# Which engine forms the low parts of the weights, scales the delta rule's key products and makes the output's residual

## The chip, the cores and the metric

The kernel runs on one core of one Trainium2 chip. The metric is the device time of one execution in microseconds (us), as a median of several runs. Engines are named as in the profile: PE is TensorE's matmul, PEld its weight load, DVE is VectorE, ACT is ScalarE, POOL is GpSimd, SP is SyncE, which issues the DMAs.

## What is computed

One layer of a streaming encoder trunk, for 2048 prompt frames and 32 sample frames, 1024 wide. The normalised input `h` goes through one wide projection; its columns feed two branches, and the branches are merged, projected and added to `h`:

```python
qa, ka, va, za, qkv_b, zb, a_b, b_b, gate_a, gate_b = split_projection(x @ w_in)
ya = (oa.reshape(bsz, t, A_WIDTH) * jax.nn.silu(za)) @ w_branch_a   # oa: chunk-band softmax attention
yb = (ob * jax.nn.silu(zb)) @ w_branch_b                            # ob: gated delta rule, chunks of 64
mix = jax.nn.sigmoid(gate_a) * ya + jax.nn.sigmoid(gate_b) * yb
y = layer_norm(ALPHA * x + mix @ w_out, ln_g, ln_b)
```

The delta rule of branch B carries a 64x64 state per head from chunk to chunk:

```python
v_new = u_c - jnp.einsum('bhld,bhde->bhle', w_c, s)
o_c = (jnp.einsum('bhld,bhde->bhle', q_c * jnp.exp(gc_c)[..., None], s)
       + jnp.einsum('bhij,bhje->bhie', qk_c, v_new))
s = s * jnp.exp(g_last)[..., None, None] + jnp.einsum('bhld,bhle->bhde', k_dec, v_new)
```

## The kernel before

**The projection** runs as 49 jobs per half of the prompt (the sample frames ride with the second half). A job is a block of 128 columns of `w_in` (one job holds the 16 columns of `a` and `b`). To keep float32's accuracy in fast float16 matmuls, weights and `h` are both split into a high and a low float16 part, and a job multiplies high by high, low weights by high, and high by low (`multiply`). The weights' two parts are made per job by `divide`, half a tile (128x512) at a time: in the first half of the prompt ACT squares the tile, a matmul with a constant tile (`b<-w_sq,tiny`, in `power`) sums the squares over the partitions, and a power of two, `w_scale`, comes out; then ACT scales the raw tile in place (`wraw<-wraw,w_scale`, 128x1024), ACT casts each half to float16 (`whi`), and POOL subtracts that from the scaled tile (`wlo<-wraw,whi`, line 645).

**The order of the jobs** is fixed in `all_jobs`: a few jobs of the merge gates (`HEAD`), the `a`/`b` job, then `ORDER`: branch B's jobs (q, k, v, z of four pairs of heads) with gate jobs strewn in, then `TAIL` gate jobs, then branch A's. So the half of the prompt falls into a stretch with the delta rule (about 150 to 500 us and 950 to 1310 us) and one with attention (about 500 to 800 and 1310 to 1650). After 1650 us the branches are projected, merged and put through `w_out` in blocks of 256 frames (`merge`).

**The delta rule** (`phase_b`): DVE solves the triangular systems by substitution, 62 small operations per block of 512 frames (`substitute`, tiles `sys_t` and `sys_u`). Then `chain` steps through the chunks, two chains at a time: PE multiplies the state (`x<-state`), DVE forms `r` from it, PE multiplies `r` by the inverse (`x<-r`), DVE scales that by a factor per row (`vn<-x,sc`, line 1335), PE multiplies `vn` (`x<-vn`), and DVE updates the state (`state<-state,sc,x`). 132 such steps in all.

**The residual** (`x_load`): for each of 17 tiles of 128 rows (the last has 32), `xt` is fetched, DVE takes off the mean and multiplies by the inverse deviation (128x1024, two factors per row), and POOL multiplies by the row of gains and adds the row of offsets (`l0g`, `l0b`; for the first two tiles DVE does). In the same stretch `evac` and `fold` of `merge` do the gates on DVE (`sg<-sg,a`, `sg<-sg`), cast on ACT (`mh`), and leave the low part to DVE and POOL in turn (`ml`).

**What sets the order** on each engine is a planner inside the kernel. Every piece of work is a generator (a stream) with a clock; `Flow` always resumes the stream with the earliest clock, and the engine wrappers (`V`, `S`, `G`, `PE`) add a price per instruction and keep a busy time per engine (`Flow.spend`). The queues of the engines are what this yields, and each engine works its queue in order. A call on `nc.vector` instead of `V` goes into DVE's queue at that point but costs the plan nothing.

## Time and profile before

| | us |
|---|---|
| runs before, median of 3 | 2088.36 (2082.26, 2088.36, 2091.96) |
| profiled execution | 2083.65 |
| its span | 2081.6 |
| PE busy | 1968.6 (95%) |
| DVE busy | 1499.7 (72%) |
| ACT busy | 978.1 (47%) |
| POOL busy | 633.1 (30%) |

The span is the time from the first to the last instruction of the program in the profiled execution; 2 us of that execution lie outside it. Busy shares are means over the stages, and DVE's busy time holds time in which an instruction has started and stands still. The profiled execution is 4.7 us below the median of the runs.

### The profile page before, as it was taken

To read this page: it belongs to the slowest core of one execution; us is meant where nothing else is said; L and a number is where in the kernel's file an instruction comes from. 1 tells how busy PE (TensorE), PEld (TensorE's weight loads), DVE (VectorE), ACT (ScalarE), POOL (GpSimd) and SP (SyncE) were. 2 spreads that over 40 slices of the span, in tenths; PEclk is the share of its full clock that TensorE was granted. 3 is DMA by queue.
4 is the path that set the end of the run, shared out by engine and by line. 5 is a ranking of instruction groups with operands and counts; after the bars stand their busy time and mean duration, and the time that the engine had idled before them with its cause. 6 is when DMAs were issued, how large, how long until landed. Compare 5 with 4: busy or idle time off the path is not lost. (4 is left out here: it accounts for less than half of the span.)

```text
span 2081.6 us, 41386 instructions
## 1 busy us (share of the span) xinstructions
PE 1968.6 (95%) x15098; PEld 1411.3 (68%) x15098; DVE 1499.7 (72%) x4661; ACT 978.1 (47%) x2098; POOL 633.1 (30%) x708
## 2 busy tenths in 40 slices
PE   4999999999999999998999999999999988999998
PEld 3454666766465657566667777667666777888996
DVE  7679889873377758679998986356656667666775
ACT  5565554444466667564544543355656641111110
POOL 6244333422312113243332331311011134433342
PEclk9999999999999999999999999999999999999999
DMA  3233232323423233122233233332232445433331
GB/s 119 72 92 106 75 102 57 100 80 91 116 86 111 70 92 100 65 85 72 66 89 83 77 99 84 105 92 76 72 88 88 129 137 175 132 102 122 102 116 54
DMA packets 197719, 196.49 MB, mean 94 GB/s; under 512 B 79622, under 2 KB 147570, under 8 KB 197516
## 3 DMA queue, kind: packets, MB, share of 16 engines
q1 hardware_dynamic: 197516, 193.85, 31.6%
q8 instruction: 119, 1.95, 0.4%
q14 instruction: 84, 0.69, 0.1%
HBM read 135.91 MB, written 50.53 MB: 90 GB/s over the span
## 5 line engine op out<-in xcount | busy, mean ns | idle before, releaser
L260 PE MATMUL pj<-hi,whi 128*128 128x512 f16 (+2 forms) x1992 | 644.8, 339 | 10.4 <-DVE zb L260 2.7
L260 PE MATMUL pj<-hi,wlo 128*128 128x512 f16 (+2 forms) x1952 | 635.9, 338 | 2.4 <-POOL wlo L260 2.3
L260 PEld LDWEIGHTS <-whi 128*128 128x128 f16 x3984 | 413.5, 105 | 214.5 <-issue 3.9
L260 PE MATMUL pj<-lo,whi 128*128 128x512 f16 (+2 forms) x1992 | 457.7, 340 | 0.0
L260 POOL TENSOR_TENSOR wlo<-wraw,whi 128x512 f16<-128x512 f32 x192 | 226.9, 1184 | 585.9 <-ACT whi L260 313.0
L260 PEld LDWEIGHTS <-wlo 128*128 128x128 f16 x1952 | 204.8, 105 | 111.1 <-issue 10.7
L260 ACT CAST mh<-sg 128x256 fp32r<-128x256 f32 x64 | 25.9, 406 | 279.6 <-DVE sg L260 279.6
L260 ACT CAST ph<-b 128x512 f16<-128x512 f32 (+2 forms) x224 | 93.1, 421 | 100.0 <-PE b L260 96.8
L260 DVE TENSOR_TENSOR pl<-b,ph 128x512 f16<-128x512 f32 (+2 forms) x224 | 107.7, 485 | 44.7 <-ACT ph L260 43.1
L260 PE MATMUL a<-ghi,whi 128*128 128x256 f32 (+1 forms) x512 | 132.6, 290 | 6.3 <-DVE sg L260 6.2
L260 DVE TENSOR_TENSOR sys_u<-sys_u,sys_t 128x60 f32<-128x60 f32 (+23 forms) x527 | 129.3, 251 | 6.7
L260 ACT ACTIVATE wraw<-wraw,w_scale 128x1024 f32<-128x1024 f32 (+1 forms) x98 | 111.5, 1138 | 46.6 <-DVE w_scale L260 42.9
L260 PE MATMUL a<-ghi,wlo 128*128 128x256 f32 (+1 forms) x512 | 130.3, 285 | 0.0
L260 ACT CAST whi<-wraw 128x512 f16<-128x512 f32 (+1 forms) x196 | 119.4, 612 | 20.9 <-PE pj L260 18.0
L260 DVE TENSOR_TENSOR sys_t<-sys_u,sys_p 128x60 f32<-128x60 f32 (+21 forms) x459 | 121.2, 265 | 6.1
L260 ACT ACTIVATE sb<-sb,mx,unit 128x640 f32<-128x640 f32 (+4 forms) x128 | 108.8, 851 | 20.0 <-DVE mx L260 19.7
L260 DVE SCALAR_TENSOR_TENSOR acc<-raw,cwT,acc 128x512 f32<-128x512 f32 x144 | 114.0, 792 | 5.4 <-ACT acc L260 4.4
L260 POOL TENSOR_TENSOR w_scale<-w_scale,mhalf 128x1 f32<-128x1 f32 x49 | 30.9, 631 | 269.3 <-DVE w_scale L260 204.2
L260 PE MATMUL b<-ident,sb 128*128 128x128 f32 x560 | 100.6, 279 | 5.3 <-ACT sb L260 2.2
L260 PEld LDWEIGHTS a<-ghi,whi 128*128 128x128 f32 x512 | 98.0, 191 | 9.0 <-DVE sg L260 7.8
L260 ACT COPY v_t<-o 128x64 f32<-128x64 f32 x132 | 27.7, 210 | 161.1 <-PE o L260 133.3
L260 PEld LDWEIGHTS a<-ghi,wlo 128*128 128x128 f32 x512 | 97.8, 191 | 0.3
(350 smaller groups left out, 4221.8 us busy)
## 6 DMA issues: line engine op xcount, KB each, us to landing
wraw<-in_w_in SPq DMA_DIRECT2D x192, 256.0 KB
sg<-sig SPq DMA_DIRECT2D x112, 128.0 KB
sig<-sig SPq DMA_DIRECT2D x44, 256.0 KB
sys_p<-sol_p SPq DMA_DIRECT2D x17, 512.0 KB
x<-in_x_p SPq DMA_DIRECT2D x16, 512.0 KB
xt<-in_x_p SPq DMA_DIRECT2D x16, 512.0 KB
out_y_p<-xt SPq DMA_DIRECT2D x16, 512.0 KB
glo<-g SPq DMA_DIRECT2D x14, 512.0 KB
```

Source lines behind the costliest of these rows:

```text
L260: r = f(*a, **k)
```

## The change

Four edits:

- **Jobs get a mark, `delta`**: those of `ORDER` without the `a`/`b` job, the three `HEAD` jobs of the second half, and four of six `TAIL` jobs in each half: 25 jobs in the first half of the prompt, 28 in the second. The others (first jobs, branch A's, the last gates) are divided as before.
- **`divide` of a marked job**: ACT no longer scales the raw tile; it casts each half with the scale as a pointer operand (`whi<-wraw,w_scale`), and DVE forms the low half as scale times raw minus high (line 649 of the changed kernel) where POOL subtracted. The instruction is issued on `nc.vector`, and the plan books 0.7 us for it on a resource `W` of its own, not on DVE. In the first half the power sum's matmul is planned 1.0 us later.
- **`vn` of the chain** is formed by ACT, with the factor as its scale, not by DVE.
- **The residual** is formed by DVE alone, as subtract-then-multiply and multiply-then-add on halves of 512 columns (4 instructions per tile), with the row tiles as second tensor; POOL does none of it.

```diff
--- before.py
+++ after.py
@@ -575,7 +575,7 @@
         def __init__(self, half, wid, src, evac=None, key=None, cols=P, blocks=None):
             self.wid = wid
             self.half, self.src, self.evac, self.cols, self.key = half, src, evac, cols, key
-            self.end = self.two = False
+            self.end = self.two = self.delta = False
             self.blocks = blocks or BLOCKS[half]
 
     NRAW = 2
@@ -631,18 +631,28 @@
             yield t
             if job.half == 0:
                 S.activation(out=hi[:], in_=raw[:], func=AF.Square, accum_out=w_sq[:])
-                yield
+
+                yield flow.cur.clock + (1.0 if job.delta else 0.0)
                 yield from power(sc, w_sq[:])
                 flow.start(factors(job.wid))
             src, main = raw[:, :, 0:job.cols], hi[:, :, 0:job.cols]
-            S.activation(out=src, in_=src, func=AF.Copy, scale=sc)
+            if not job.delta:
+                S.activation(out=src, in_=src, func=AF.Copy, scale=sc)
             for i in range(2):
                 ks = slice(4 * i, 4 * i + 4)
-                S.copy(out=main[:, ks], in_=src[:, ks])
-                yield
 
                 rest_ = lo[:, ks] if job.cols == P else hi[:, ks, job.cols:P]
-                G.tensor_tensor(out=rest_, in0=src[:, ks], in1=main[:, ks], op=ALU.subtract)
+                if job.delta:
+
+                    S.activation(out=main[:, ks], in_=src[:, ks], func=AF.Copy, scale=sc)
+                    yield
+                    nc.vector.scalar_tensor_tensor(out=rest_, in0=src[:, ks], scalar=sc, in1=main[:, ks],
+                                                   op0=ALU.mult, op1=ALU.subtract)
+                    flow.spend("W", 0.7)
+                else:
+                    S.copy(out=main[:, ks], in_=src[:, ks])
+                    yield
+                    G.tensor_tensor(out=rest_, in0=src[:, ks], in1=main[:, ks], op=ALU.subtract)
                 if i:
                     raw_gate.give()
                     q_w.put((job, hi, lo))
@@ -1332,7 +1342,7 @@
                     flow.start(outputs(k.qb[:, c, :], st, os_))
                     yield
                     vn = bp.tile([P, HD], F32, tag=f"vn{xn}", bufs=2, name="vn")
-                    V.tensor_scalar(out=vn[:], in0=ys, scalar1=sc[:, 1, c:c + 1], scalar2=None, op0=ALU.mult)
+                    S.activation(out=vn[:], in_=ys, func=AF.Copy, scale=sc[:, 1, c:c + 1])
                     yield
                     PE.matmul(ds_, k.kdb[:, c, :], vn[:], start=True, stop=True)
                     flow.start(outputs(k.qkb[:, c, :], vn[:], os_, vc, k.out if c == k.nch - 1 else None))
@@ -1919,18 +1929,24 @@
 
     def all_jobs():
         for half in range(2):
-            for what in [None] * HEAD[half] + ["ab"] + ORDER:
+            for n, what in enumerate([None] * HEAD[half] + ["ab"] + ORDER):
                 if what is None:
-                    yield rest[half].pop(0)
+                    job = rest[half].pop(0)
+                    job.delta = half == 1 or n >= HEAD[0]
+                    yield job
                 elif what == "ab":
                     yield Job(half, 48, [(0, w_ab[:, :, 0:NH]), (32, w_ab[:, :, NH:2 * NH])], key=(1, None, 0), cols=HD,
                               blocks=AB_BLOCKS[half])
                 else:
                     p, i = what
                     wid = (16 + 4 * i if i < 3 else 28) + p
-                    yield Job(half, wid, [(0, w_in[wid])], key=(1, p, i))
-            for _ in range(TAIL[half]):
-                yield rest[half].pop(0)
+                    job = Job(half, wid, [(0, w_in[wid])], key=(1, p, i))
+                    job.delta = True
+                    yield job
+            for n in range(TAIL[half]):
+                job = rest[half].pop(0)
+                job.delta = n < TAIL[half] - 2
+                yield job
             for p in range(NP):
                 for i, f in enumerate((8, 4, 0, 12)):
                     yield Job(half, f + p, [(0, w_in[f + p])], key=(0, p, i))
@@ -2171,13 +2187,12 @@
         w.st = fp.tile([P, 2, 6], F32, tag="fst", bufs=3, name="fst")
         yield dma(xt[:rows], x_s if rows < P else x_p[gt * P:(gt + 1) * P, :])
         yield rows_ready
-        V.tensor_scalar(out=xt[:rows], in0=xt[:rows], scalar1=mv[:rows, gt, 0:1],
-                        scalar2=mv[:rows, gt, 1:2], op0=ALU.subtract, op1=ALU.mult)
-        yield
-        eng = V if gt < 2 else G
-        eng.tensor_tensor(out=xt[:rows], in0=xt[:rows], in1=rowv["l0g"][:rows], op=ALU.mult)
-        yield
-        eng.tensor_tensor(out=xt[:rows], in0=xt[:rows], in1=rowv["l0b"][:rows], op=ALU.add)
+        for name, q, op0, op1 in (("l0g", 0, ALU.subtract, ALU.mult), ("l0b", 1, ALU.mult, ALU.add)):
+            for c in range(2):
+                cs = slice(c * 512, (c + 1) * 512)
+                V.scalar_tensor_tensor(out=xt[:rows, cs], in0=xt[:rows, cs], scalar=mv[:rows, gt, q:q + 1],
+                                       in1=rowv[name][:rows, cs], op0=op0, op1=op1)
+                yield
         w.ready.done()
 
     def finish(w, gt, rows, c, ps, end):
```


Where it moves instructions. First VectorE's queue in the second half, beside one chunk's `r` (`sys_t` and `sys_u` are the substitution, `q_bd` and `v` belong to other blocks). Before:

```order
L260 TENSOR_TENSOR sys_t<-sys_u,sys_p 128x6x11
L260 TENSOR_TENSOR sys_u<-sys_u,sys_t 128x6x11
L260 TENSOR_TENSOR sys_t<-sys_u,sys_p 128x6x10
L260 TENSOR_TENSOR sys_u<-sys_u,sys_t 128x6x10
L260 TENSOR_TENSOR sys_t<-sys_u,sys_p 128x6x9
L260 TENSOR_TENSOR q_bd_10325<-qk_11413,ex 64x8x64
L260 TENSOR_TENSOR sys_u<-sys_u,sys_t 128x6x9
L260 SCALAR_TENSOR_TENSOR r<-x,negc,v_t_10363 128x64
L260 SCALAR_TENSOR_TENSOR v_12730<-e,acc 128x512
```

And after the change, at the same rows of the substitution:

```order
L260 TENSOR_TENSOR sys_t<-sys_u,sys_p 128x6x11
L260 SCALAR_TENSOR_TENSOR v_12647<-e,acc 128x512
L260 TENSOR_TENSOR sys_u<-sys_u,sys_t 128x6x11
L649 SCALAR_TENSOR_TENSOR wlo<-wraw,w_scale,whi 128x512
L260 SCALAR_TENSOR_TENSOR r<-x,negc,v_t_10335 128x64
L260 TENSOR_TENSOR sys_t<-sys_u,sys_p 128x6x10
L260 TENSOR_TENSOR sys_u<-sys_u,sys_t 128x6x10
L260 TENSOR_TENSOR sys_t<-sys_u,sys_p 128x6x9
L260 TENSOR_TENSOR sys_u<-sys_u,sys_t 128x6x9
L260 SCALAR_TENSOR_TENSOR state<-state,sc,x 128x64
```

A low part of the weights (L649), which stood in POOL's queue, now stands directly ahead of `r`, and `r` comes two rounds of the substitution earlier; 52 of the 106 such instructions stand between the first and the last chain step of a half, 18 of them at most two rows ahead of an `r` or a `state`.

Next ScalarE's queue, at the same block of the delta rule (`v_t<-o` copies a chunk's result out, `e` and `acc` are the convolution's, `zb` and `raw` empty a projection bank). Before, with the scaling of a whole raw tile and its two casts:

```order
L260 COPY k_bd_10309<-qk_12159 64x8x64
L260 ACTIVATE wraw<-wraw,w_scale 128x1024
L260 CAST whi<-wraw 128x512
L260 ACTIVATE zb<-pj,w_half 128x272
L260 ACTIVATE p_c_10360<-qk_12159 128x512
L260 COPY v_t_10363<-o 128x64
L260 CAST whi<-wraw 128x512
L260 COPY v_t_10363<-o 128x64 x2
```

After:

```order
L260 ACTIVATE vn<-x,sc 128x64
L260 COPY v_t_10335<-o 128x64
L260 ACTIVATE whi<-wraw,w_scale 128x512
L260 ACTIVATE raw_12506<-pj,w_inv 128x240
L260 ACTIVATE raws_12508<-pj,w_inv 128x32
L260 ACTIVATE vn<-x,sc 128x64
L260 ACTIVATE e<-acc 128x512
L260 ACTIVATE whi<-wraw,w_scale 128x512
L260 COPY v_t_10335<-o 128x64
L260 ACTIVATE vn<-x,sc 128x64
L260 COPY v_t_10335<-o 128x64
```

The scaling of the tile is gone, the cast carries the factor, and each chunk's `vn` stands among the other work, behind whatever is queued ahead of it.

Last VectorE's queue in one block of the merge. Before:

```order
L260 TENSOR_TENSOR ml<-sg,mh 128x256
L260 TENSOR_SCALAR xt<-xt,mv 128x1024
L260 SCALAR_TENSOR_TENSOR sg<-sg,a 128x256
L260 TENSOR_TENSOR sg<-sg 128x256
L260 SCALAR_TENSOR_TENSOR sg<-sg,a 128x256
L260 TENSOR_TENSOR sg<-sg 128x256
L260 TENSOR_TENSOR ml<-sg,mh 128x256
L260 SCALAR_TENSOR_TENSOR sg<-sg,a 128x256 x2
L260 TENSOR_TENSOR sg<-sg 128x256
```

After:

```order
L260 TENSOR_TENSOR ml<-sg,mh 128x256
L260 SCALAR_TENSOR_TENSOR xt<-xt,mv,l0g 128x512
L260 SCALAR_TENSOR_TENSOR sg<-sg,a 128x256
L260 TENSOR_TENSOR sg<-sg 128x256
L260 SCALAR_TENSOR_TENSOR sg<-sg,a 128x256
L260 SCALAR_TENSOR_TENSOR xt<-xt,mv,l0g 128x512
L260 TENSOR_TENSOR sg<-sg 128x256
L260 SCALAR_TENSOR_TENSOR xt<-xt,mv,l0b 128x512
L260 TENSOR_TENSOR ml<-sg,mh 128x256
L260 SCALAR_TENSOR_TENSOR xt<-xt,mv,l0b 128x512
```

The residual's halves (`xt<-xt,mv,l0g` and `l0b`) stand between the gates' instructions; POOL's queue has none of them left.

## Rows read from the trace of the kernel before

**Rows 1.** Busy time by stretch: us, each engine (instructions), TensorE clock, DMA share, GB/s.

```profile
150.00:500.00 350.00, 331.82 (x2493) 220.62 (x2492) 290.51 (x1091) 171.16 (x350) 118.79 (x150) 0.99 0.32 88
950.00:1310.00 360.00, 339.42 (x2987) 256.08 (x2987) 309.37 (x1133) 162.93 (x375) 112.30 (x147) 0.99 0.31 82
```

**Rows 2.** TensorE waits, 150 to 500 us: releaser, us in total, times, longest.

```profile
PE x L260 <- DVE r L260: 5.6, 6, 2.3
PE x L260 <- DVE state L260: 2.6, 5, 0.9
PE x L260 <- DVE vn L260: 2.4, 4, 0.9
```

**Rows 3.** TensorE waits, 950 to 1310 us.

```profile
PE x L260 <- DVE r L260: 9.0, 11, 1.4
...
PE x L260 <- DVE state L260: 2.2, 5, 0.8
...
PE x L260 <- DVE vn L260: 1.3, 4, 0.6
```

**Rows 4.** Timeline from 1045.8 us: start, us, engine, line, operation, tiles, [idle before, releaser].

```profile
1045.84 1.16 POOL L260 TENSOR_TENSOR wlo<-wraw,whi 128x512 f16<-128x512 f32 x1 [1.04 <-ACT whi L260]
1045.94 1.13 DVE L260 TENSOR_TENSOR sys_u<-sys_u,sys_t 128x60 f32<-128x60 f32 x1
...
1047.96 0.27 DVE L260 SCALAR_TENSOR_TENSOR r<-x,negc,v_t 128x64 f32<-128x64 f32 x1
...
1048.29 0.43 PE L260 MATMUL x<-r,u_bd 128*128 128x64 f32 x2 [1.43 <-DVE r L260]
```

**Rows 5.** Tiles sys_u and sys_t: count, duration ns min/median/max, first and last start.

```profile
L260 DVE TENSOR_TENSOR sys_u<-sys_u,sys_t x527: 147/211/1221, 143.7 to 1279.9; 128x60 f32<-128x60 f32 x17, 128x48 f32<-128x48 f32 x13, 128x66 f32<-128x66 f32 x11, 128x54 f32<-128x54 f32 x11
L260 DVE TENSOR_TENSOR sys_t<-sys_u,sys_p x459: 130/216/1224, 148.6 to 1279.7; 128x54 f32<-128x54 f32 x30, 128x72 f32<-128x72 f32 x17, 128x75 f32<-128x75 f32 x17, 128x60 f32<-128x60 f32 x17
```

**Rows 6.** The page, costliest groups: count, busy us, mean ns, idle before it.

```profile
L260 DVE TENSOR_TENSOR sys_u<-sys_u,sys_t 128x60 f32<-128x60 f32 (+23 forms) x527 | 129.3, 251 | 6.7
L260 DVE TENSOR_TENSOR sys_t<-sys_u,sys_p 128x60 f32<-128x60 f32 (+21 forms) x459 | 121.2, 265 | 6.1
```

**Rows 7.** Busy time of tile wlo alone, in the stretches with chain steps.

```profile
213.00:491.00 278.00, 88.32 (x231) 28.09 (x232) 0.00 (x0) 35.31 (x30) 0.98 0.32 86
993.00:1308.00 315.00, 113.06 (x379) 43.12 (x379) 0.00 (x0) 35.87 (x31) 0.99 0.31 82
```

**Rows 8.** Tile acc: VectorE's three-operand form with a pointer scalar, ns min/median/max.

```profile
L260 DVE SCALAR_TENSOR_TENSOR acc<-raw,cwT,acc x144: 711/744/1698, 87.4 to 1175.4; 128x512 f32<-128x512 f32 x144
```

**Rows 9.** VectorE's groups by shape: count, busy us, mean ns, idle before it.

```profile
L260 DVE TENSOR_SCALAR vn<-x,sc 128x64 f32<-128x64 f32 x132 | 37.0, 280 | 19.5 <-PE x L260 17.6
L260 DVE TENSOR_TENSOR sg<-sg 128x256 f32<-128x256 f32 x56 | 54.6, 979 | 0.8
```

**Rows 10.** ScalarE's groups by shape.

```profile
L260 ACT CAST whi<-wraw 128x512 f16<-128x512 f32 x192 | 118.0, 616 | 20.8 <-PE pj L260 18.0
L260 ACT ACTIVATE wraw<-wraw,w_scale 128x1024 f32<-128x1024 f32 x96 | 110.1, 1146 | 46.6 <-DVE w_scale L260 42.9 <-DVE rs L260 2.0 <-DVE sys_u L260 1.3
L260 ACT ACTIVATE acc<-raw,cwT 128x512 f32<-128x512 f32 x48 | 34.5, 719 | 15.2 <-DVE qk L260 7.5 <-DVE v L260 2.7 <-DVE qk_s L260 1.9
L260 ACT COPY v_t<-o 128x64 f32<-128x64 f32 x132 | 27.7, 210 | 161.1 <-PE o L260 133.3
```

**Rows 11.** TensorE's group of the weights' power sum, with what ended its waits.

```profile
L260 PE MATMUL b<-w_sq,tiny 128*128 128x1 f32 x98 | 17.1, 244 | 6.9 <-ACT whi L260 5.7 <-DVE kd_bd L260 1.2
```

**Rows 12.** ScalarE's waits, 950 to 1310 us.

```profile
ACT e L260 <- DVE acc L260: 30.9, 19, 3.6
```

**Rows 13.** Tile xt on GpSimd, and tile sg on VectorE, 1700 us to the end.

```profile
L260 POOL TENSOR_TENSOR xt<-xt,l0g x15: 2389/2395/2518, 1738.9 to 2034.3; 128x1024 f32<-128x1024 f32 x14, 32x1024 f32<-32x1024 f32 x1
L260 DVE TENSOR_TENSOR sg<-sg x61: 411/426/2607, 1704.1 to 2045.2; 128x256 f32<-128x256 f32 x53, 128x288 f32<-128x288 f32 x8
```

**Rows 14.** TensorE waits, 1738 us to the end.

```profile
PE a L260 <- DVE sg L260: 3.2, 3, 1.9
```


## The prediction

> **What bounds the kernel now.** I read the busy time by stretch first, then what TensorE waits for in the stretches that the change touches, then one such wait in the timeline. In both stretches with the delta rule PE is busy 95% and 94% of the time (331.82 of 350 us, 339.42 of 360) [rows 1]: PE is the bound, its matmuls stay the same, and the change can win only the 18.2 and 20.6 us in which PE stands still there, and the like elsewhere. DVE is busy 83% and 86% in the same stretches, ACT 49% and 45% [rows 1]. Of PE's 38.8 idle us, 10.6 in the first half (5.6 + 2.6 + 2.4) and 12.5 in the second (9.0 + 2.2 + 1.3), 23.1 in all, are waits of the chain's matmuls for DVE: for `r`, `state` and `vn` [rows 2, 3].
>
> Why DVE is late, one wait shows [rows 4]: POOL's subtraction for a weight tile starts at 1045.84 and takes 1.16 us; a small `sys_u` operation that DVE starts 0.10 us later takes 1.13 us and ends with it; `r` comes at 1047.96, and PE has stood for 1.43 us. The same tile's operations have a median of 211 ns and reach 1221, those of `sys_t` 216 and 1224 [rows 5]. So a DVE operation on two SBUF tensors stands while POOL works on such a subtraction. With the means of 251 and 265 ns [rows 6], 527 x 40 ns = 21.1 us and 459 x 49 ns = 22.5 us lie above the medians: 43.6 us of standing in these two groups, an estimate since their shapes differ. All groups together can't stand longer than POOL's subtractions last: 35.31 + 35.87 = 71.2 us in the two stretches with chain steps, 61 of them [rows 7].
>
> **The change part by part.** The sum is made against the profiled execution, 2083.65 us; the median of the runs is 4.7 us higher, and I add that at the end.
>
> *Low parts on DVE.* They leave POOL, and the 43.6 us of standing go with them. In their place come 106 operations with three operands and a pointer scalar on 128x512. `acc` is that form: 711 ns at least, 744 in the median [rows 8]; I take 744. In the changed order 52 of them stand between the first and the last chain step of a half: 52 x 0.744 = 38.7 us. The plan counts them on a resource of their own, not on DVE; neither did it count the standing. So 43.6 us of unplanned time on DVE become 38.7, in the same queue and ahead of the same `r` and `state`. The waits of 23.1 us scale to 23.1 x 38.7 / 43.6 = 20.5.
>
> *`vn` leaves DVE*: 132 x 0.280 = 37.0 us [rows 9]. DVE's load in the two stretches goes from 599.9 to 599.9 - 43.6 + 38.7 - 37.0 = 558.0 of 710 us, its free share from 15.5% to 21.4%. A late DVE catches up that much sooner, so I take 20.5 x 15.5 / 21.4 = 14.8 us. Saved: 23.1 - 14.8 = **8.3 us**. The ends are 0 (the new operations delay as the old standing did, and the plan, which knows that `vn` is gone, packs the steps closer) and 23.1 (every wait goes).
>
> *On ACT*, per marked job, the scaling of 1.146 us goes, and two casts grow from 0.616 us to 0.719, the price of `acc<-raw,cwT`, which carries a pointer scale [rows 10]: 53 x (1.146 - 0.206) = 49.8 us less. `vn` adds 132 of 128x64 from PSUM: the plain copy of that shape takes 0.210 us, with the same 0.103 for the pointer 0.313, so 41.3 us more. ACT's load stays. What counts is how long `vn` takes after its matmul. The instruction is 33 ns longer than on DVE, 132 x 0.033 = 4.4 us if PE stood for every one; PE waited at 8 of the 132 [rows 2, 3]. An engine's queue costs a late comer about its busy share times half an instruction: ACT's mean is 171.16 / 350 = 0.49 us, so 0.49 x 0.245 = 0.12 us; DVE's is 290.51 / 1091 = 0.27 us, so 0.83 x 0.135 = 0.11 us [rows 1]. That is even. I take **+1 us**, between 0 and 4.4; the case of a blocked queue is a rival below.
>
> The Trainium skill, *ScalarE: Activation LUTs*, "Rules for kernel authors", speaks against this edit: it gives adding and multiplying to VectorE, not ScalarE. Its figures in "What ACT_TABLE_LOAD costs" (186 ns, 0.833 per element, 93 per pointer operand) make an estimate of 332 ns for this `vn`, which would put 6.9 us in the place of the 4.4. The rows here show a smaller difference, 0.313 against 0.280, and a DVE that is fuller than ACT, so I keep the rows.
>
> *The power sum 1.0 us later.* PE stood 5.7 us in front of it for ACT's squares, in the first half of the prompt [rows 11]. An added microsecond of planned distance covers most waits of that size, though not those ahead of unmarked jobs: **-3 us**, between 0 and -5.7.
>
> *The residual.* POOL's multiplications with `l0g` take 2.4 us each and start at 1738.9 us [rows 13]; the gates' `sg<-sg` on DVE has a median of 426 ns but reaches 2607 [rows 13], with a mean of 979 over 56 [rows 9]: 56 x 0.553 = 31 us of standing in one group. That goes. DVE gets four operations per tile of about 0.74 us, 17 x 4 x 0.74 = 50 us at most, where it had one pass of the tile. It is a fair trade for DVE, and for PE only 3.2 us of waits for `sg` lie after 1738 us [rows 14], part of them at the start, where POOL isn't the cause. I take **-2 us**, between 0 and -3.2.
>
> Raw tiles come free earlier and the weights' parts are ready sooner, since a step of 1.146 us is gone; PE hardly waits for them now, so this costs and gives nothing. Elsewhere the new order shifts work by a few instructions; I take 0. The two delta stretches show a granted clock of 0.99 [rows 1], 7 us at most to win or lose with fewer or more stops.
>
> Sum: -8.3 + 1 - 3 - 2 = -12.3, so 2083.65 - 12.3 = 2071.4, and with 4.7 for the median **2076 us**.
>
> **The rivals.**
>
> 1. *One for one.* The new operations on DVE delay the chain just as the standing did: 18 of the 52 stand at most two rows ahead of an `r` or a `state`, and the plan reckons with none. Then the 23.1 us stay, and only -3 - 2 + 1 is left: 2083.65 - 4 + 4.7 = 2084 us. For it: unplanned time falls only from 43.6 to 38.7 us. Against it: the standing may be up to 71.2 us, and DVE loses 37 us of other work.
>
> 2. *All of it.* The standing is what made PE wait, and without it the plan holds: -23.1 - 5.7 - 3.2 = -32 us, so 2083.65 - 32 + 4.7 = 2056 us. For it: the wait in the timeline has POOL's operation right ahead of it [rows 4]. Against it: the new operation takes 0.74 us in the same place, where the standing took 1.13 - 0.21 = 0.92. The Trainium skill, *SBUF — State Buffer*, "Who interferes with whom", says that a VectorE instruction with two SBUF inputs and a GpSimd instruction that reads SBUF exclude each other for the whole instruction. By that rule the trace agrees (1.13 us beside 1.16), all standing behind a subtraction ends, but the new operation, with two SBUF inputs itself, can be held by what POOL still does.
>
> 3. *Slower: `vn` gets stuck in ACT's queue.* ACT works in order, and it stands at the convolution's tanh until DVE has made `acc`: 19 times in the second half's stretch, 30.9 us, 1.6 us each [rows 12]. A `vn` behind such an instruction stands as long, and so does its chain. With as many in the first half, 38 x 1.6 = 62 us; if half of them have a `vn` behind them, PE loses 31 us against the 5 that the other edits give: 2083.65 + 31 - 5 + 4.7 = 2114 us. It decides from 15 us on, that is when one in four does. Against it: after `r` the next step was as exposed to DVE's own queue before.
>
> **How the numbers follow.** A measurement of this kernel can tell about 0.5% (10.4 us) from no change; the runs before lie 9.7 us apart. Chances: the forecast 0.41, one for one 0.28, all of it 0.17, slower 0.14. Faster by over 0.5% means under 2078: all of rival 2 and 0.33 of the forecast, together 0.50. Within 0.5%: 0.08 of the forecast, 0.27 of rival 1, 0.02 of rival 3, together 0.37. Slower: 0.01 and 0.12, together 0.13. The range goes from rival 2's 2056 to 2096: rival 1 plus the 4.4 us of `vn` and the 7 us of clock; beyond it lie most of rival 3 and little of rival 2, under 0.2.
>
> **What would show it.** In the profile after: PE's waits for `r` and `state` in the two stretches near 13 us, and for a `vn` on ACT near 2; the maximum of `sys_u` and `sys_t` seldom above 1 us and their means near the medians; the new `wlo` on DVE at 0.71 to 0.75 us; `sg<-sg` near 0.43 us; the wait for the squares under 3 us. I am wrong if `r` waits as long as before with a `wlo` right ahead of it (rival 1), if waits for `vn` on ACT exceed 15 us (rival 3), or if PE's idle time moves elsewhere, into waits for weights or at the changes of stretch.

## The result, and the profile after

| | median us | runs | ratio to before, 95% interval |
|---|---|---|---|
| before | 2087.93 | 13 (2077.27 to 2091.96) | |
| after | 2094.38 | 13 (2090.52 to 2101.38) | 1.0043 [1.0031, 1.0056] |

The change makes the kernel slower by 0.43%, 9 us by the ratio. That is less than the 0.5% that I called no change, and inside my range, but on the other side of zero from the forecast of 2076. The profiled execution took 2101.26 us (span 2099.5), 7 us above the median; the one of before took 2083.65. Below, every time is given as ratio x 2087, as microseconds above or below before, since each group of runs had its own runs of before beside it.

In the two stretches with the delta rule nearly all went as forecast. TensorE's waits (releaser, us, times, longest), 150 to 500 us and then 950 to 1310 us, against [rows 2, 3]:

```profile
PE b L260 <- ACT p_c L260: 6.2, 2, 5.7
PE x L260 <- DVE state L260: 5.6, 6, 2.1
PE x L260 <- ACT vn L260: 1.4, 2, 0.8
...
PE x L260 <- DVE r L260: 0.9, 3, 0.4
```

```profile
PE x L260 <- DVE r L260: 4.4, 9, 1.1
PE x L260 <- DVE state L260: 3.8, 6, 0.9
```

`r`, `state` and `vn` together fall from 23.1 to 16.1 us, where I had forecast 14.8 and 1 for `vn`. The page's groups (count, busy us, mean ns, idle before), and under them two of the groups by shape, answer to [rows 6, 9, 10, 11]:

```profile
L260 DVE TENSOR_TENSOR sys_u<-sys_u,sys_t 128x60 f32<-128x60 f32 (+23 forms) x527 | 112.4, 218 | 7.8
...
L260 DVE TENSOR_TENSOR sys_t<-sys_u,sys_p 128x60 f32<-128x60 f32 (+20 forms) x459 | 99.5, 219 | 6.7
...
L260 ACT ACTIVATE whi<-wraw,w_scale 128x512 f16<-128x512 f32 x106 | 75.5, 716 | 45.9 <-DVE w_scale L260 27.3
L260 ACT ACTIVATE vn<-x,sc 128x64 f32<-128x64 f32 x132 | 41.2, 312 | 119.1 <-PE x L260 118.4
```

```profile
L260 DVE TENSOR_TENSOR sg<-sg 128x256 f32<-128x256 f32 x56 | 26.7, 477 | 0.7
```

```profile
L260 PE MATMUL b<-w_sq,tiny 128*128 128x1 f32 x98 | 16.1, 233 | 2.3 <-ACT whi L260 1.9 <-DVE ss L260 0.4
```

`sys_u` and `sys_t` lose most of their standing (means 251 and 265 before, now 218 and 219), the cast takes 716 ns (forecast 719), `vn` 312 (forecast 313), `sg<-sg` 477 instead of 979, and the squares keep PE for 1.9 us instead of 5.7. The new `wlo` on DVE has a median of 745 ns (forecast 744).

And yet the time rose. The busy time by stretch (engines, granted clock, DMA share, GB/s) shows where; first after, then the one stretch of before that [rows 1] leaves out:

```profile
150.00:500.00 350.00, 331.30 (x2483) 224.30 (x2482) 279.08 (x1081) 170.70 (x394) 76.41 (x111) 0.96 0.32 87
800.00:950.00 150.00, 129.67 (x990) 88.00 (x989) 104.42 (x229) 82.64 (x166) 23.92 (x48) 0.93 0.24 74
950.00:1310.00 360.00, 343.85 (x2974) 255.18 (x2972) 308.14 (x1129) 166.27 (x415) 76.39 (x123) 0.99 0.30 82
```

```profile
800.00:950.00 150.00, 143.29 (x1111) 98.75 (x1110) 110.13 (x247) 96.78 (x190) 58.03 (x85) 0.99 0.26 82
```

Between 800 and 950 us, where one half of the prompt gives way to the other and no chain step runs, PE is busy 13.6 us less, at a granted clock of 0.93 instead of 0.99. From 150 to 500 us it is busy as long as before, but the clock is 0.96 instead of 0.99, up to 10.5 us over 350. That part can't be laid to the marks or the clearing: e1 and e6 (below) have the same instructions in the same order on every engine up to 800 us, at a clock of 0.98 and 0.99, and the last `x<-r` of the first half starts at 506.4 us in after, 499.5 in e1 and 497.8 in e6. So some 7 to 9 us of this one execution, itself 7 us above the median, come from neither. The first chain step of the second half starts at 1040 us, 29 us later than before's 1011; from there to the end after is 11 us faster.

Most of the 13.6 us is one wait. DVE's timeline and then PE's after (start, us, engine, line, operation, tiles, [idle before, releaser]):

```profile
850.32 0.91 DVE L260 MEMSET k_bd<- 128x1024 f32 x1 [0.16 <-issue]
...
867.50 0.91 DVE L260 MEMSET u_bd<- 128x1024 f32 x1 [0.16 <-issue]
868.33 1.28 DVE L649 SCALAR_TENSOR_TENSOR wlo<-wraw,w_scale,whi 128x512 f16<-128x512 f32 x2
```

```profile
857.88 0.38 PE L260 MATMUL pj<-hi,whi 128*128 128x512 f16 x1
869.01 0.61 PE L260 MATMUL pj<-hi,wlo 128*128 128x512 f16 x1 [10.75 <-DVE wlo L649]
```

When the second half opens its buffers, DVE clears 17 diagonal tiles, 1.07 us from one to the next, 850.3 to 868.4 us. The low parts of the first two marked tiles of that half were formed before it (809.9 to 822.8 us); the third marked tile has both of its low parts behind the clearing in DVE's queue, and PE stands 10.75 us for them. Before, DVE cleared from 838.9 to 856.9 us, and POOL formed the two low parts of that tile beside it, at 842.1 and, here in its timeline, at 845.2; PE waited 0.38 us for the second:

```profile
845.24 1.16 POOL L260 TENSOR_TENSOR wlo<-wraw,whi 128x512 f16<-128x512 f32 x1 [1.94 <-ACT whi L260]
```

The other new wait is 5.7 us for `p_c` at 192 us. Two lines of ACT's timeline and one of DVE's show its source: DVE stands 3.81 us for a transfer (`sys_p`), `sc` is queued behind it, ACT stands 4.28 us for `sc`, and `p_c` comes last of what queued up on ACT.

```profile
188.38 0.21 ACT L260 ACTIVATE sc<-sc 128x8 f32<-128x8 f32 x1 [4.28 <-DVE sc L260]
...
191.69 0.61 ACT L260 ACTIVATE p_c<-qk 128x512 f32<-128x512 f32 x1
```

```profile
186.76 0.24 DVE L260 TENSOR_SCALAR sys_t<-sys_p,sys_u 128x31 f32<-128x31 f32 x1 [3.81 <-DMA sys_p<-sol_p]
```

### The profile page after: what moved, and what is told of

It is laid out like the page before. It is cut to its first block, busy times and chain, and to the rows that moved or that the text cites. A ratio compares the mean times of both kernels' runs of the same rounds, so it can differ in the third digit from the quotient of the medians.

```text
span 2099.5 us, 41323 instructions
## 1 busy us (share of the span) xinstructions
PE 1979.9 (94%) x15098; PEld 1418.5 (68%) x15098; DVE 1474.8 (70%) x4682; ACT 969.1 (46%) x2177; POOL 437.0 (21%) x572
## 5 line engine op out<-in xcount | busy, mean ns | idle before, releaser
L260 PE MATMUL pj<-hi,whi 128*128 128x512 f16 (+2 forms) x1992 | 651.0, 341 | 14.7 <-POOL whi L260 3.5
L260 PE MATMUL pj<-hi,wlo 128*128 128x512 f16 (+2 forms) x1952 | 643.3, 342 | 13.6 <-DVE wlo L649 10.8
L260 POOL TENSOR_TENSOR wlo<-wraw,whi 128x512 f16<-128x512 f32 x86 | 99.5, 1160 | 345.0 <-issue 199.0
L260 DVE TENSOR_TENSOR sys_u<-sys_u,sys_t 128x60 f32<-128x60 f32 (+23 forms) x527 | 112.4, 218 | 7.8
L260 DVE SCALAR_TENSOR_TENSOR acc<-raw,cwT,acc 128x512 f32<-128x512 f32 x144 | 108.6, 754 | 6.8 <-ACT acc L260 5.7
L260 DVE TENSOR_TENSOR sys_t<-sys_u,sys_p 128x60 f32<-128x60 f32 (+20 forms) x459 | 99.5, 219 | 6.7
L260 ACT ACTIVATE whi<-wraw,w_scale 128x512 f16<-128x512 f32 x106 | 75.5, 716 | 45.9 <-DVE w_scale L260 27.3
L260 ACT ACTIVATE vn<-x,sc 128x64 f32<-128x64 f32 x132 | 41.2, 312 | 119.1 <-PE x L260 118.4
L260 DVE CUSTOM_DVE_ANT_0 sb<-a,bias 128x320 f32<-128x320 f32 (+4 forms) x128 | 61.8, 486 | 44.8 <-PE a L260 43.9
```

Source lines behind the costliest of these rows:

```text
L260: r = f(*a, **k)
```

## Experiments

Theory A: the loss is the marking of the second half's first three tiles, whose low parts stand behind the clearing. Rival B: `vn` on ACT and low parts on DVE stop PE more often in the first half. Rival C: any new order of the instructions brings such stops. (The expectations speak of 20 cleared tiles and of the first of the three; the trace shows 17, and the third.)

### The three tiles and the clearing

**e1**, the changed kernel without these marks:

```
-                    job.delta = half == 1 or n >= HEAD[0]
+                    job.delta = n >= HEAD[half]
```

> The changed kernel, but the first three weight tiles of the second half of the prompt stay unmarked: POOL forms their low parts, as in the kernel before. Theory A (the loss sits at the change of halves: the low part of the first of these tiles stands on DVE behind the clearing of 20 tiles at about 0.9 us each, PE stops once for 10.8 us there and runs part of the next stretch at the lower clock): the wait for wlo near 869 us goes, the window 800 to 950 us gets back about 14 us of PE idle time and some 6 us of clock, and the time falls by 12 to 20 us from the changed kernel's 2094, to 2074 to 2082. Theory B (the loss is spread: vn on ACT and low parts on DVE make PE stop more often in the first half, where the granted clock fell from 0.99 to 0.96): the time stays at 2088 to 2096, whatever happens at 869 us. Theory C (the loss is what any new order of the instructions can bring, tied to no part): the time moves by a few us in either direction, and the stretches that the edit doesn't touch change as much as the one that it does.

Measured: 0.9948 [0.9931, 0.9965], 10.9 us faster than before and 19.9 faster than after. From the last `x<-r` of the first half to the first of the second, after takes 533.7 us and e1 514.1, 19.6 less: the whole gain lies there. The stretch, beside after's 129.67 and 0.93:

```profile
800.00:950.00 150.00, 144.33 (x1123) 100.14 (x1121) 119.98 (x276) 91.34 (x182) 39.95 (x71) 0.99 0.26 81
```

**e5**, the kernel before with these three tiles marked and nothing else changed (`job.delta = half == 1 and n < HEAD[1]`, `vn`, residual and power sum as before):

> The kernel before with one thing alone: the first three weight tiles of the second half are marked, so DVE forms their six low parts and ACT scales in the cast; all other tiles, vn, the residual and the power sum as before. Theory A (a low part that stands on DVE behind the clearing of 20 tiles stops PE): one PE wait for wlo of about 11 us near 855 us, the granted clock in 800 to 950 us at 0.93 instead of 0.99, nothing won elsewhere: 2085 + 11 + 6 = 2102, between 2096 and 2106. Theory C (new order as such): within 5 us of 2085, with no long wait.

Measured: 1.0083 [1.0069, 1.0098], 17.3 us slower. PE's longest wait between 800 and 950 us:

```profile
PE pj L260 <- DVE wlo L649: 13.2, 1, 13.2
```

**e6**, the changed kernel, all tiles marked, the clearing of the second half on POOL:

```
-                V.memset(t[:], 0.0)
+                (G if half else V).memset(t[:], 0.0)
```

> The changed kernel, all its tiles marked, but in the second half POOL clears the 20 diagonal tiles, not DVE. Theory A in its narrow form (the clearing ahead of the low part on DVE is the cause, not that DVE forms it): the wait near 869 us shrinks to under 1 us and the time comes down like that of the kernel with the three tiles unmarked, to 2072 to 2082. Rival (DVE is a worse place for the low parts of these tiles whatever stands ahead): the time stays above 2088.

Measured: 0.9971 [0.9959, 0.9983], 6.1 us faster than before, 15.1 faster than after. POOL's and DVE's timelines:

```profile
844.26 3.64 POOL L260 MEMSET qk_bd<- 128x1024 f32 x4
847.84 2.75 POOL L260 MEMSET q_bd<- 128x1024 f32 x3
```

```profile
845.50 0.75 DVE L649 SCALAR_TENSOR_TENSOR wlo<-wraw,w_scale,whi 128x512 f16<-128x512 f32 x1 [5.13 <-ACT whi L260]
```

In e6 PE works the same matmuls in the same order as in after, to the end, so the two traces can be laid side by side: at the same matmul after is 10.6 us behind just ahead of its stop, 22.9 us behind at 872.4 us and 22.6 at the last matmul. So the stop and the first matmuls behind it cost 12.4 us, and the rest of the way adds nothing; 9.8 of the 10.6 us were there before the clearing began, in the same queues.

Theory A holds from three sides: marking the three tiles costs 17 us alone, 20 in the changed kernel and 28 between e16 and e3 (below), and it is the clearing ahead of two of the six low parts, not their being on DVE, that costs. The stop is 11 to 13 us of it; where the rest comes from stays open. The clearing on POOL doesn't stretch the low part beside it: 0.75 us, its median. The Trainium skill, *SBUF — State Buffer*, "Who interferes with whom", says that a VectorE instruction with two SBUF inputs contends with a GpSimd instruction that reads SBUF, not with one that only writes it; these two rows agree.

**e17**, the changed kernel with the low parts booked on DVE in the plan (`V.scalar_tensor_tensor`, where the change issues them past the plan and books 0.7 us on a resource "W" that no engine has):

> The changed kernel, the same instructions on the same engines, but the plan counts the low parts on DVE instead of on a resource of their own. If the booking is the cause: the plan sees the first low part of the second half come late, puts other work on PE ahead of it, and the wait near 869 us falls to under 3 us: 2076 to 2084. If the clearing's place is the cause (all clearings are issued in one go, so nothing can go between them, and the weight tiles are multiplied in order): the wait stays at 10 to 13 us, 2088 to 2100.

Measured: 1.0107 [1.0093, 1.0122], 22.3 us slower than before, 13 slower than after, at a clock of 0.970 to 0.974. The wait is 13.2 us again. The booking isn't the cause of the stop: the kernel issues the clearings in one go, and nothing goes between them. The time is above the 2088 to 2100 that I expected of this case. **e18**, the same booking in the fastest kernel (e11, below):

> The fastest kernel so far (low parts on DVE but for the first three tiles of the second half, residual on DVE, vn on DVE, no later power sum: 2064) with the low parts booked on DVE. If unplanned time on DVE still delays the chain of the delta rule there: 2054 to 2060. If PE's waits for r, state and vn (16 us in the two stretches) are what the chain's length leaves in any order: 2060 to 2070.

Measured: 0.9945 [0.9931, 0.9958], 10.6 us slower than without the booking. Both halves of what I expected from honest booking failed; new stops came elsewhere (`v_t` on POOL 4.9 us, `vf` on ACT 4.6), and why the unbooked order is better stays open.

### The parts alone

**e3**, low parts with all their marks, alone (`vn`, residual and power sum as before):

> The kernel before with one part alone: low parts of the marked weight tiles on DVE and the scaling in ACT's casts; vn stays on DVE, the residual on POOL, the power sum's planned distance as before. Theory A: the stop of about 11 us at the change of halves is there, and the time is above the kernel before by 5 to 12 us (11 us of stop and some 6 of clock, less what r and state win, which my sum put at 20.5 of 23.1 left, so 3): 2093 to 2100. Theory B (vn on ACT is the cause): no loss, 2080 to 2088. Theory C: a few us either way.

Measured: 1.0053 [1.0033, 1.0072], 11.1 us slower, with a wait for `wlo` of 11.5 us at 861. As A said. **e16**, the same without the three marks:

> The kernel before with low parts on DVE and the scaling in ACT's casts alone, the first three tiles of the second half left to POOL; vn, the residual and the power sum as before. By the runs so far (2064 with the residual, which alone is worth 11.6): 2073 to 2077, a gain of 9 to 13 us. By my prediction's working (waits from 23.1 to 20.5): 2082 to 2084. In the trace the waits for r and state in the two stretches with the delta rule should then be near 8 us in all by the first, near 18 by the second.

Measured: 0.9921 [0.9904, 0.9939], 16.5 us faster, more than either figure. PE's busy time in the two stretches:

```profile
150.00:500.00 350.00, 333.19 (x2488) 221.78 (x2485) 292.02 (x1130) 156.26 (x334) 78.19 (x112) 0.98 0.32 89
...
950.00:1310.00 360.00, 343.66 (x3018) 259.52 (x3017) 297.64 (x1157) 149.40 (x357) 73.09 (x112) 0.99 0.31 84
```

PE stands still for 16.8 and 16.3 us there, 5.6 less than before [rows 1]. The waits for `r`, `state` and `vn` are 9.5 and 8.3, 5.3 less. For `r` and `state` alone, of which I expected near 8 or near 18, they are 12.8: between the two, and the time is below both. The span of the profiled execution is 11.4 us shorter than before's: 5.6 of idle time in the two stretches, 1.2 between 800 and 950 us (144.48 us busy), and 4.6 in small pieces elsewhere. The median gained some 5 us more than this one execution.

**e7**, the residual alone:

> The kernel before with one part alone: the output's residual as four operations with three operands on DVE, none on POOL. My sum gave it 2 us of gain, between 0 and 3.2: 2080 to 2085 with the kernel before at 2084. If low parts and vn bring nothing and the residual is what wins in the kernel with the three tiles unmarked (2075): 2076 to 2079. The stretch from 1700 us on is the only one that may change in its operations; a change ahead of that would be order alone.

Measured: 0.9942 [0.9926, 0.9958], 12.1 us faster. Up to 1661 us PE has the same matmuls in the same order, within 2.2 us of before; from the first `a<-ghi` matmul to the last matmul PE takes 401.5 us instead of 412.4. Before and then alone, nearly that stretch:

```profile
1661.00:2073.00 412.00, 395.72 (x2554) 350.06 (x2552) 282.37 (x494) 74.94 (x191) 152.04 (x122) 0.98 0.37 118
```

```profile
1662.00:2063.00 401.00, 389.39 (x2553) 348.65 (x2552) 268.75 (x541) 75.14 (x191) 79.21 (x92) 0.99 0.37 121
```

The same matmuls take 6.3 us less busy time, of which the clock (0.98 to 0.99) can be 4, and 4.7 us less idle time. DVE, which does POOL's work on top, is busy 13.6 us less: `sg<-sg` falls from 979 to 466 ns.

**e4**, `vn` on ACT alone:

> The kernel before with one part alone: vn on ACT, 132 times. Theory A: DVE loses 37 us of work in the two stretches with the delta rule, the waits for r and state fall by some us, and nothing stops at the change of halves: 2080 to 2088. Theory B: p_c waits some 5 us more on ACT, the clock in the first half falls as in the changed kernel, and the time rises by 5 to 10 us to 2093 to 2098. Theory C: a few us either way.

Measured: 1.0038 [1.0023, 1.0052], 7.9 us slower. **e9**, the same move without telling the plan, so that every queue keeps the order of before:

```
-  V.tensor_scalar(out=vn[:], in0=ys, scalar1=sc[:, 1, c:c + 1], scalar2=None, op0=ALU.mult)
+  nc.scalar.activation(out=vn[:], in_=ys, func=AF.Copy, scale=sc[:, 1, c:c + 1])
+  flow.spend("V", 0.125 + HD / 960.0)
```

> The kernel before with vn on ACT, but counted by the plan as if it stayed on DVE: every engine's instructions keep the order of before, and only vn changes its engine. (With the plan told, vn alone made 2093, 8 us more than before.) If what that kernel lost comes from vn's place on ACT (a vn behind other ACT work): about 2093 here too, with waits for vn on ACT above the 3.7 us of before. If it comes from the plan's new order, which has no room for what it doesn't count: 2078 to 2085, and waits for r and state smaller than 14.5 and 4.8 us, since DVE has 37 us less to do in the same order.

Measured: 1.0035 [1.0020, 1.0051], 7.3 us slower, in the old order. Its waits, and ACT's timeline ahead of one of them:

```profile
PE x L260 <- ACT vn L1335: 17.0, 24, 1.5
...
PE x L260 <- DVE r L260: 11.8, 11, 4.2
PE x L260 <- DVE state L260: 6.5, 12, 1.3
```

```profile
309.38 1.15 ACT L260 ACTIVATE wraw<-wraw,w_scale 128x1024 f32<-128x1024 f32 x1 [0.47 <-DVE w_scale L260]
310.56 0.62 ACT L260 CAST whi<-wraw 128x512 f16<-128x512 f32 x1
311.09 0.62 ACT L260 ACTIVATE p_c<-qk 128x512 f32<-128x512 f32 x1
311.74 0.32 ACT L1335 ACTIVATE vn<-x,sc 128x64 f32<-128x64 f32 x1
```

My third rival, at half its size: `vn` makes PE wait 17.0 us instead of 3.7, here (1.42 us) behind the scaling and the cast of a weight tile and a `p_c`, while `r` gets only 2.7 us back. In e4 the plan knew of the move, and PE hardly waits for `vn` (0.2 us), although ACT still scales: the plan decides on these waits. The loss is as large all the same, and stays open: `state` makes PE wait 9.9 us instead of 4.8 and `sg` 9.9 instead of 6.2, but `r` and `vn` give 8.8 us back, and `p_c` (2.5 us, before 4.1) is not what theory B made it; of the 11.0 us that the profiled execution takes longer, 6.3 are PE's own busy time. In the changed kernel the scaling is gone, and PE waits 1.4 us for `vn`. **e2**, the changed kernel with `vn` back on DVE:

> The changed kernel with vn back on DVE (the plan counts it there again). Theory A: 2092 to 2098, since the stop of 10.8 us at the change of halves stays and the waits for r and state rise by some of the 8 us that my sum gave to vn's leaving. Theory B in the form that vn on ACT delays ACT's other work (p_c, for which PE waited 5.75 us at 192): the wait for p_c falls to about 1 us, the clock in 150 to 500 us comes back to 0.99, and the time falls by about 10 us to 2084. Theory C: a few us either way.

Measured: 1.0073 [1.0048, 1.0098], 6.2 us slower than after, with intervals that overlap. The wait for `p_c` stays (5.2 us), so `vn` on ACT isn't its cause. In the kernel without the three marks and without the later power sum the same move is worth 0.4 us (e8 against e11, below), inside their intervals.

### The later power sum

**e8** is e1 without the added microsecond (`yield` in place of `yield flow.cur.clock + ...`); **e10** is before with that microsecond alone:

> The changed kernel with the first three tiles of the second half unmarked (2075 us), and without the added microsecond ahead of the power sum. If that microsecond is what put PE's wait of 5.4 us for p_c at 192 us (ACT stands for sc, which stands on DVE behind an operation whose transfer lands 3.4 us after the plan's time): the wait falls to 3 us or less and the time by 2 to 6 us, against 2 to 3 us of waits for the squares that come back: 2070 to 2077. If the added microsecond is worth the 3 us that my sum gave it: 2077 to 2080, with PE's waits for whi ahead of the power sum near 5.7 us again, where they are 2.5 now.

> The kernel before with one thing alone: the power sum of the marked tiles planned 1 us later. My sum gave this 3 us of gain; taken away from the kernel with the three tiles unmarked it gave 9 us (2075 to 2066), against that. Forecast by the prediction: 2082, the waits for whi ahead of the power sum from 5.7 to under 3 us. By the run that took it away: 2088 to 2095, later parts of each weight tile, and a longer stretch up to the first chain step of the first half (214.5 us before).

Measured: e8 0.9896 [0.9881, 0.9911], 10.8 us faster than e1; e10 1.0100 [1.0081, 1.0118], 20.9 us slower than before; both moves are larger than any that I had expected. The waits for the squares in e10 do fall, from 5.7 to 2.6 us; I had that right. In e8 the wait for `p_c` at 185 us is 2.9 us instead of e1's 5.4, and DVE's waits for `sys_p` 1.7 instead of 7.7 (in before, without the microsecond, they are 7.3 too, so they don't come from it alone). In e10 PE's busy time is spread thinner over the whole first half, beside before's 117.86, [rows 1] and 297.04:

```profile
0.00:150.00 150.00, 112.08 (x630) 65.59 (x631) 101.44 (x243) 84.57 (x149) 64.92 (x82) 0.97 0.28 90
150.00:500.00 350.00, 324.83 (x2388) 215.41 (x2387) 293.52 (x1090) 170.45 (x344) 117.08 (x151) 0.97 0.30 85
500.00:800.00 300.00, 291.48 (x2156) 171.49 (x2155) 179.50 (x676) 172.35 (x356) 66.59 (x70) 0.99 0.30 92
```

18.3 us of busy time are missing by 800 us. Up to there PE's waits are up to 5.6 us for `ab`, 4.9 for `v_t` on POOL and 4.1 for `vf`, which before shows none of, and to 4.9 from 1.9 for `wlo` on POOL. Three more sizes of the same edit on the kernel before:

> The kernel before with the power sum of the marked tiles planned 0.1 us later (1.0 us alone cost 22 us). If the loss grows with the added time: 2 to 4 us, 2087 to 2090. If it is the new order as such: anywhere from 2075 to 2108, without relation to the size.

> The same with 0.5 us. If the loss grows with the added time: about 11 us, 2094 to 2100, and the last chain step of the first half (509 us before, 537 with 1.0) near 520 us. New order as such: anywhere from 2075 to 2108.

> The same with 2.0 us. If the loss grows with the added time: 30 us and more, 2115 to 2135. New order as such: anywhere from 2075 to 2108, without relation to the size.

| added, us | ratio, 95% interval | us |
|---|---|---|
| 0.1 | 1.0007 [0.9996, 1.0018] | +1.5 |
| 0.5 | 1.0012 [1.0002, 1.0023] | +2.5 |
| 1.0 | 1.0100 [1.0081, 1.0118] | +20.9 |
| 2.0 | 1.0050 [1.0033, 1.0067] | +10.4 |

The loss doesn't grow with the added time, and the smallest can't be told from zero. It is what each new order brings (rival C); none of the four orders was better than the old one. Which single move in the order of 1.0 us starts the chain of stops wasn't found.

### What is fastest

**e11** is e8 with `vn` back on DVE (low parts without the three marks, and the residual); **e12** is e6 without the later power sum:

> The kernel of 2066 us (first three tiles of the second half unmarked, no later power sum) with vn back on DVE; so low parts on DVE and the residual alone. If vn on ACT helps once POOL's low parts are gone, as in the changed kernel, where taking it back cost 5 us: 2069 to 2073. If it hurts as it did alone (8 us): 2058 to 2063. By my sum the vn part of 8.3 was 5.7 less 1: 2070.

> The changed kernel with all its tiles marked, the 20 diagonal tiles of the second half cleared by POOL, and no later power sum. If the two losses found (the clearing ahead of the low part, the later power sum) are separate and add: 2079 less the same 9 us, 2067 to 2072, as the kernel with the three tiles unmarked came to 2066. If the later power sum's loss hung on the order that went with the unmarked tiles: 2075 to 2080.

Measured: e11 2063.71 us, 0.9894 [0.9875, 0.9913], 22.1 us faster than before, and e8, 2065.89, can't be told from it; both beat both kernels. e12 0.9932 [0.9914, 0.9951], 8.1 us better than e6: the two losses add nearly as expected.

## Why the prediction went wrong

One path through the runs takes the kernel before to the changed one in five steps, all against their own runs of before. A time against before is known to 3 or 4 us, a step between two of them to some 5:

| step | kernel | us against before | this step | forecast for it |
|---|---|---|---|---|
| low parts, three tiles unmarked | e16 | -16.5 | -16.5 | -2.6 alone |
| residual | e11 | -22.1 | -5.6 (-12.1 alone) | -2 |
| `vn` on ACT | e8 | -21.7 | +0.4 (+7.9 alone) | -5.7 and +1 |
| power sum 1 us later | e1 | -10.9 | +10.8 (+20.9 alone) | -3 |
| the three tiles marked | after | +9.0 | +19.9 (+17.3 alone) | 0 |

The prediction failed where it took 0 for what the new order does outside the stretches that it had priced: the last two steps cost 30.7 us, for which it had a gain of 3, and outweigh the 21.7 us that the first three win.

- *Standing on DVE behind POOL*: right in place and in kind. `sys_u`, `sys_t` and `sg<-sg` lost it, the new operation costs 745 ns, and the waits for `r`, `state` and `vn` fell from 23.1 to 16.1 us.
- *Low parts* were mis-sized: 16.5 us for a term of 2.6. The waits that I scaled fell by only 5.3 us, twice my figure; the rest lies in small pieces outside the stretches that I counted, and no run ties it to a mechanism of the edit.
- *The residual*, right in kind (the rows of `sg<-sg`), was mis-sized at 2 of 12.1 us alone. I bounded it by PE's waits for `sg`, 3.2 us. The runs show 10.9 us in the time of the same matmuls, more than half of it in their own busy time, which a table of waits doesn't carry.
- *`vn`* was even in the end, not a gain of 4.7. Rival 3's waits come where the plan isn't told of the move (17.0 us in e9); told of it, PE waits 0.2 us for `vn` in e4, where ACT still scales, and 1.4 in after.
- *The power sum* is the first step that failed in sign. I priced the wait that it takes away, rightly, and wrote of the rest: "Elsewhere the new order shifts work by a few instructions; I take 0." One order cost 20.9 us alone; the others between 1.5 and 10.4.
- *The marks of the second half's start* are the step that I didn't price. I counted the 106 low parts by the stretches with chain steps, 52 of them, and wrote that the weights' parts would be "ready sooner" and that "this costs and gives nothing"; I didn't ask what stands on DVE ahead of the other 54. Ahead of two of them stood 17 clearings, and PE stopped for 10.75 us. The last sentence of the prediction, "at the changes of stretch", names the place and gives it no number.
- *The clock*: "7 us at most to win or lose" was meant for two stretches. Over all runs of after the granted clock is 0.975 to 0.982, over those of before in the later groups 0.982 to 0.991; the 0.008 between their middles is 17 us of 2090 at most. Without the stop it is 0.982 to 0.987 in e1 and e6, and 0.986 to 0.991 in e11. It also differs between executions of one order (0.96, 0.98 and 0.99 from 150 to 500 us in after, e1 and e6); no run here changes the clock alone.

The signs of success that I had listed came out near their forecasts (`r` and `state` together 14.7 us against 13), and the total didn't: they all lie where the change was expected to help. The last sign of being wrong, idle time that moves to the changes of stretch, came out as well.

## What to carry to other kernels

When an operation moves to another engine, list for each of its instances what stands ahead of it in the new engine's queue, above all at the changes of stage, where clearing and other set-up is issued in one go; the marks of three tiles, one of them behind 17 clearings, cost 17 to 28 us, where the low parts of the other 50 tiles won 16.5. In a kernel whose order a planner makes, a moved planned time is a new order of the whole: give such an edit a range from runs with several sizes of it, here from nothing to 21 us, rather than the price of the one wait that it covers. And test a bundle part by part: this one held 22 us of gain and 31 us of loss.

## What the runs showed of the hardware

- Seventeen clearings of 128x1024 f32 take 18.1 us on DVE (0.91 us each, 1.07 from one to the next) and 15.3 us on POOL in e6 (four in 3.64 us), and those on POOL didn't stretch DVE's low part with two SBUF inputs beside them (0.75 us).
- After the stop of 10.75 us the clock is at its lower level for the first matmuls and then back: the 128x512 matmuls start 0.43 us apart up to 872 us and 0.21 us apart from then on. The seven intervals at the lower level cost 1.5 us. By stretches of 10 us the granted clock is 0.75, 0.59 and 0.90 from 850 to 880 us, and in the one with 0.59 PE is busy only 0.99 us: there the lower clock costs nearly nothing. The lower level was there ahead of the stop as well: the 128x272 matmuls start 0.23 us apart up to 853.5 us and 0.12 us apart from 855.1 on.

```profile
850.00:860.00 10.00, 8.26 (x49) 5.67 (x47) 8.38 (x11) 3.24 (x7) 1.39 (x4) 0.75 0.09 28
860.00:870.00 10.00, 0.99 (x3) 0.44 (x4) 8.48 (x10) 0.00 (x0) 0.42 (x1) 0.59 0.00 0
870.00:880.00 10.00, 10.00 (x62) 6.03 (x60) 0.00 (x0) 1.17 (x2) 0.00 (x0) 0.90 0.27 87
```

- DVE with the residual's four operations per tile is busy 13.6 us less than with one, in the same stretch: the 56 `sg<-sg` alone, which no longer stand beside POOL, take 28.7 us less (979 to 466 ns each).
